# Scores and weighting of an attention mixer two to three pieces later, pooled products in four banks

## The chip, the cores and the metric

One core of a Trainium2 chip runs the whole kernel. The core has five engines, each with its own queue of instructions: TensorE (PE, matrix products; its loads of weights are shown as PEld), VectorE (DVE), ScalarE (ACT), GpSimd (POOL) and SyncE (SP), which here only starts DMAs. DMAs are also started from GpSimd's queue. The metric is the time of the program on the device in microseconds (us), the median of several runs.

## The reference

An encoder of two layers over 256 tokens of 1024 channels, in float32. Each layer has a token mixer and a gated MLP:

```python
def _token_mixer(xn, w_in, w_pool, pool_scale, w_a, w_b, w_o, rel_bias):
    u, q, k, v, g_pool, g_attn = jnp.split(xn @ w_in, SPLITS, axis=-1)
    ug = u.reshape(B, S, POOL_GROUPS, POOL_GROUP_DIM)
    pooled = jnp.stack([_centred_mean(ug[:, :, gi], w) for gi, w in enumerate(POOL_WINDOWS)], axis=2) - ug
    pool_out = jnp.einsum('bsgc,gcd->bsgd', pooled, w_pool).reshape(B, S, POOL_WIDTH) * pool_scale
    ...
    # three groups of four heads with keys at steps of 1, 4 and 16 tokens; per group: logits, lse, p, o
    wts = jax.nn.softmax(jnp.stack(lses, axis=0), axis=0)
    attn = jnp.einsum('gbsh,gbshd->bshd', wts, jnp.stack(outs, axis=0).astype(jnp.float32))
    merged = jax.nn.sigmoid(g_pool) * (pool_out @ w_a) + jax.nn.sigmoid(g_attn) * (attn_out @ w_b)
    return merged @ w_o

for layer in range(DEPTH):
    h = h + _token_mixer(_rmsnorm(h, norm1[layer]), ...)
    h = h + _conv_ffn(_rmsnorm(h, norm2[layer]), ...)
return _rmsnorm(h, norm_f)
```

The softmax over each group followed by the weighting of groups by their denominators is one softmax over the keys of all three groups, and the kernel computes it so.

## The kernel before

**Split operands.** TensorE multiplies operands of a shorter format (fp32r). To keep float32's precision, an operand is split into a high part (a cast on ScalarE) and the rest (a subtraction on VectorE), and a product is three: high by high, high by rest, rest by high. Names ending in `h` and `l`, or `th` and `tl`, are such pairs.

**Weights in pieces.** The class `Weights` (object `W`) brings all weights in one fixed order. A load from memory (`raw`, three buffers, started by SyncE) holds two pieces; a piece is split into `wh` (L208, ScalarE) and `wl` (L210, VectorE), five buffers each, and then multiplied. `W.get()` hands out the next piece, and has the splits made up to `W.look` pieces ahead (3, and 4 in the mixer's attention). `queue_behind(insts, n)` makes the next `n` splits stand behind the given instructions in the queues of ScalarE and VectorE; the last four such requests are kept. A piece in the projections by tokens (`by_tokens`, tile `t_ps`) is twelve products of 512 columns.

**The mixer's order.** After the values `v` and the pooling of `u`, the mixer runs these projections one behind the other: six blocks for queries and keys (four pieces each, `t_ps`), two halves of the pooled branch by `w_a` (`po2`, four pieces each), two halves of the first gate (four pieces each), and then twice a half of the second gate (four pieces, called the third and fourth gate here) with a half of the attention's output by `w_b` (two pieces, operand `at2`).

A block of queries or keys comes out by tokens and is needed by channels, with the tokens regrouped by their steps. `cross` does this over memory: VectorE transposes (L737, tile `qk_rows`, later `turning` for probabilities), SyncE starts a store, and GpSimd starts four loads (L744, tiles `k`, `qk_rows`, `turned_p`). The first two blocks hold queries and keys of the group with step 1; the third to sixth hold those of the two groups with steps 4 and 16, for heads 0 and 1 (third and fourth) and for heads 2 and 3 (fifth and sixth).

**Attention between the pieces.** For each of four heads `hh` (three groups at once), `scores` makes the logits on TensorE (`s_ps`, two tiles) and the softmax on VectorE and ScalarE; `start_turn` sends the probabilities over memory (`cross`); `turn` splits what came back into `pth` (ScalarE, L1098) and `ptl` (VectorE, L1099); `weigh` multiplies them by the values (`o_ps`) and splits the result into `at2` (L1117, L1118). `parts` and `bring` unpack queries and keys. A table written by hand says behind which piece each step stands; place 0 is the first piece of the first block, places 24 to 31 are the pooled branch, 32 to 39 the first gate, and 40 to 43 the third gate:

```python
            21: ((scores, 0), (start_turn, 0)),
            24: ((scores, 1), (start_turn, 1)),
            28: ((turn, 0),),
            29: ((weigh, 0), (scores, 2), (start_turn, 2)),
            30: ((turn, 1),),
            31: ((weigh, 1), (scores, 3), (start_turn, 3)),
            38: ((turn, 3),),
            39: ((weigh, 3), (W.load_one, first_up[l][1])),
```

In this stretch (`manual_schedule`) TensorE, ScalarE and VectorE work in the order of the source; elsewhere a scheduler sets the order. SyncE and GpSimd have an order of their own that the scheduler sets throughout.

**Banks.** Two pools of four PSUM banks: `mmp` (tag `mm`: projections `t_ps`, and the products of the pooled groups `pool_ps`, in the second block) and `acc` (tag `acc`: scores, weighted values, values, residual sums). A block's `t_ps` takes two banks.

**The pooled branch's result** `pa` is copied out of its banks by ScalarE at the end of each half (L1197); its two halves take the places of the rests of queries and keys (`lows`) of heads 0 and 1, and of heads 2 and 3.

**The norm.** The output projection's sum goes into `h` (L468), is squared (L470), scaled (L495, `xn`), turned by TensorE (`xt_ps`) and split into `x` (L507, L508), half of the channels at a time, for tokens `t` = 0 and then `t` = 1.

Of the kernel before, what the change touches and what calls it, by code (L numbers as in the profile page):

```python
# [10 lines left out]
F32 = mybir.dt.float32  # L11
# [6 lines left out]
P = 128  # L18
D = 1024
S = 256  # L20
# [228 lines left out]
def encoder(ctx, tc, x, w_in, w_pool, pool_scale, w_a, w_b, w_o, norm1, norm2, w_up, conv_w,  # L249
            conv_b, w_down, rel_bias, norm_f, onehot, edges, out):  # L250
    nc = tc.nc
    const = ctx.enter_context(tc.tile_pool(name="const", bufs=1))
    wpool = ctx.enter_context(tc.tile_pool(name="weights", bufs=1))
    big = ctx.enter_context(tc.tile_pool(name="big", bufs=1))
# [39 lines left out]
    first_up = []  # L294
# [191 lines left out]
    def to_channels(x2, psum, g):  # L486

        tag = "acc" if psum is acc else "mm"  # L490

        def fin(t, r, xn):
            for n in range(4):
                cc = slice(n * 256, (n + 1) * 256)
                nc.vector.scalar_tensor_tensor(  # L495
                    out=xn[:, cc], in0=h[:, t, cc], scalar=r[:, 0:1], in1=g[:, cc],
                    op0=ALU.mult, op1=ALU.mult,
                )
            for n in range(2):
                pt = psum.tile([P, 4, P], F32, tag=tag, name="xt_ps")  # L500
                ks = slice(4 * n, 4 * n + 4)
                for k in range(4):
                    c0 = (4 * n + k) * P
                    nc.tensor.transpose(pt[:, k, :], xn[:, c0 : c0 + P], ident)
                oh, ol = (x2[:, ks, part, t, :] for part in (0, 1))
                last = [
                    nc.scalar.copy(out=oh, in_=pt),  # L507
                    nc.vector.tensor_sub(out=ol, in0=pt, in1=oh.bitcast(F32)),  # L508
                ]
                if n == 0:  # L510
                    yield
            if t == 1:
                W.queue_behind(last, 6)

        return fin
# [411 lines left out]
    for l in range(DEPTH):  # L927
# [89 lines left out]
        def pool_out(po2):  # L1017
            for j in range(2):
                i, (wh, wl) = W.get()
                for gg in range(2):  # L1020
                    for oc in range(2):
                        ps = mmp.tile([P, 2, S], F32, tag="mm", name="pool_ps")
                        cc = slice(oc * P, (oc + 1) * P)
                        two_sums(
                            pooled[2 * j + gg], 2,
                            (ps, lambda k: wh[:, 2 * gg + k, cc], lambda k: wl[:, 2 * gg + k, cc]),
                        )
                        c = 4 * j + 2 * gg + oc
                        sc = hps[:, l, c : c + 1]
                        po = sm.tile([P, 2, P], F32, tag="u", name="po")  # L1030
                        nc.scalar.mul(out=po, in_=halves(ps[:, 1]), mul=sc)
                        nc.vector.scalar_tensor_tensor(  # L1032
                            out=po, in0=halves(ps[:, 0]), scalar=sc, in1=po, op0=ALU.mult, op1=ALU.add
                        )
# [97 lines left out]
        def bring(half):  # L1132

            a = tmp[:, 0].rearrange("p (a c j) -> p c a j", a=8, c=4)
            nc.scalar.copy(out=q[:, half].rearrange("p c t (a j) -> p c (t a) j", j=32), in_=a)


        steps = {
            9: ((parts, 0),),
            13: ((parts, 1),),  # L1140
            17: ((bring, 0),),
            21: ((scores, 0), (start_turn, 0)),
            24: ((scores, 1), (start_turn, 1)),
            25: ((bring, 1),),
            28: ((turn, 0),),
            29: ((weigh, 0), (scores, 2), (start_turn, 2)),
            30: ((turn, 1),),
            31: ((weigh, 1), (scores, 3), (start_turn, 3)),
            36: ((turn, 2),),
            37: ((weigh, 2),),  # L1150
            38: ((turn, 3),),

            39: ((weigh, 3), (W.load_one, first_up[l][1])),
        }
        places = iter(range(40))

        def step():
            for f, hh in steps.pop(next(places), ()):
# [30 lines left out]
        at2 = big.tile([P, HPG, 2, 2, P], F32R, tag="at2", name="at2")  # L1189


        pa = []
        for n in range(2):
            ps = by_tokens(po2, 4, then=step)
            pa.append(big.tile([P, 2, 512], F32, tag=("q0", "k0")[n], name="pa"))
            for t in range(2):
                nc.scalar.copy(out=pa[n][:, t], in_=ps[t])  # L1197

        def gate(tag):
            ps = by_tokens(x2, 4, then=step if steps else None)  # L1200
# [5 lines left out]
        for n in range(2):  # L1206
            th = gate("q1")
            for t in range(2):
# [1 line left out]
                    out=pa[n][:, t], in0=th[:, t], scalar=1.0, in1=pa[n][:, t],  # L1210
                    op0=ALU.add, op1=ALU.mult,
                )
        assert not steps
        W.look = W.LOOK
        in_order_of_source.close()
        g2 = gain(norm2[l])
        m2 = big.tile([P, 2, KD, 2, P], F32R, tag="m2", name="m2")
        mh, ml = m2[:, 0], m2[:, 1]
        piece, load = first_up[l]
# [1 line left out]
        turned_rows = big.tile([P, 2, 2, 4, 4, 32], F32, tag="xn", name="turned")  # L1221
        for n, cc in enumerate(HALVES):
            th = gate("gates")
            ps = by_tokens(at2, 2, 2)
            ks = slice(4 * n, 4 * n + 4)
            y = turned_rows[:, n]
            z = big.tile([P, 2, 4, 4, 32], F32, tag=("q1", "v0")[n], name="merged")
            for t in range(2):

                with tc.issue_after((turning if t else made[1]).ins) if n + t else ExitStack():  # L1230
                    nc.vector.scalar_tensor_tensor(
                        out=th[:, t], in0=th[:, t], scalar=1.0, in1=ps[t], op0=ALU.add, op1=ALU.mult
                    )
                    nc.vector.tensor_add(out=th[:, t], in0=th[:, t], in1=pa[n][:, t])
                turning, there, made = to_chunks(
                    th[:, t], y[:, t], z[:, t], (mh[:, ks, t], ml[:, ks, t])
                )
# [182 lines left out]
```

## Time and profile before

| | |
|---|---|
| median of 3 runs | 868.67 us (869.62, 864.01, 868.67) |
| the profiled execution | 873.82 us, its span 872.0 us, TensorE's granted clock 0.997 |
| busy | TensorE 855.1 us (98%), weight loads 720.9 (83%), VectorE 664.8 (76%), ScalarE 489.8 (56%), GpSimd 105.9 (12%) |
| memory | 228 GB/s over the span |
| groups with the most time | split rests on VectorE (L210) 331.1 us, casts on ScalarE (L208) 285.4, products `t_ps` of `x` 301.6 and 187.0 |

Line numbers with L are those of the kernel before. "Busy" for TensorE counts overlapping matmuls once. A row of the timeline has the start, the time, engine, line, operation, tile and count, and in brackets the idle time before it and what ended it. A row of waits has the total, the number and the longest.

### The profile page before, as it was taken

The numbers are of one execution on the slowest core, as the hardware profiler recorded it, in microseconds if no ns is written. First come the engines' busy times: TensorE is split into PE (matmuls) and PEld (weight loads), VectorE is DVE, ScalarE is ACT, GpSimd is POOL, SyncE is SP. The second block draws the span as 40 slices with busy tenths as digits, with TensorE's granted clock in tenths as the row PEclk, the third lists the DMA queues.
The fourth block names the chain that finished last, engine by engine and source line by source line (L and its number), as shares of the span: only waits on it lengthen the run. The fifth ranks groups of instructions, "written<-read, shape, count | busy, mean of one in ns | idle before, by whom it ended". The sixth has DMA issues, their size and how long they took to land.

```text
span 872.0 us, 11540 instructions
## 1 busy us (share of the span) xinstructions
PE 855.1 (98%) x4151; PEld 720.9 (83%) x4151; DVE 664.8 (76%) x1018; ACT 489.8 (56%) x759; POOL 105.9 (12%) x226
## 2 busy tenths in 40 slices
PE   9999998999999999999999999998999999999997
PEld 8888787888888888888888878887888888888886
DVE  6998766777756988888855977587666777987884
ACT  6655543455444766666645555454544555765662
POOL 1801122210011211010000012131100122010100
PEclk9999999999999999999999999999999999999999
DMA  9686897895667978665735578988757398776641
GB/s 320 205 256 207 259 295 240 244 319 172 221 210 247 286 226 240 223 226 189 248 113 193 174 259 276 279 262 260 252 199 267 112 315 274 224 229 214 218 145 50
DMA packets 124418, 199.39 MB, mean 229 GB/s; under 512 B 6904, under 2 KB 69056, under 8 KB 124360
## 3 DMA queue, kind: packets, MB, share of 16 engines
q1 hardware_dynamic: 118056, 181.59, 63.3%
q0 software_dynamic: 6144, 16.79, 7.3%
q8 instruction: 33, 0.54, 0.3%
q10 hardware_dynamic: 160, 0.27, 0.1%
q14 instruction: 25, 0.20, 0.1%
HBM read 178.68 MB, written 19.94 MB: 228 GB/s over the span
## 4 chain that ended last, share of the span: by engine, by line
PE 80%; DMA 8%; DVE 6%; issue 2%; ACT 2%; POOL 1%; POOLq 0%; ACTq 0%; DVEq 0%
PE t_ps L690 31%; PE proj_ps L566 18%; PE v_ps L690 6%; PE res_ps L610 6%; PE res_ps L609 6%; PE res_ps L608 6%; DMA k<-crossing 4%; DMA crossing<-qk_rows 4%; PE v_ps L919 3%; DVE wl L210 2%; PE v_ps L826 1%; POOL k L744 1%; PE o_ps L1112 1%; ACT wh L208 1%; DVE qk_rows L737 1%
## 5 line engine op out<-in xcount | busy, mean ns | idle before, releaser
L210 DVE TENSOR_TENSOR wl<-raw,wh 128x1024 fp32r<-128x1024 f32 x274 | 331.1, 1220 | 110.6 <-ACT wh L208 94.5
L208 ACT CAST wh<-raw 128x1024 fp32r<-128x1024 f32 x274 | 285.4, 1051 | 153.5 <-PE t_ps L690 102.1
L690 PE MATMUL t_ps<-wh,x 128*128 128x512 f32 x960 | 301.6, 391 | 0.0
L690 PEld LDWEIGHTS t_ps<-wh,x 128*128 128x128 f32 x960 | 180.7, 188 | 37.6
L690 PE MATMUL t_ps<-wl,x 128*128 128x512 f32 x480 | 187.0, 390 | 0.0
L566 PE MATMUL proj_ps<-x,wh 128*128 128x512 f32 x448 | 106.5, 390 | 0.0
L690 PEld LDWEIGHTS t_ps<-wl,x 128*128 128x128 f32 x480 | 90.4, 188 | 18.6
L566 PEld LDWEIGHTS proj_ps<-x,wh 128*128 128x128 f32 x448 | 83.1, 188 | 16.6
L608 PE MATMUL res_ps<-wh,actq 128*128 128x512 f32 (+1 forms) x184 | 70.1, 381 | 0.0
L609 PE MATMUL res_ps<-wl,actq 128*128 128x512 f32 (+1 forms) x184 | 70.0, 380 | 0.0
L610 PE MATMUL res_ps<-wh,actk 128*128 128x512 f32 (+1 forms) x184 | 69.9, 380 | 0.0
L566 PEld LDWEIGHTS proj_ps<-x,wl 128*128 128x128 f32 x448 | 56.8, 191 | 2.2 <-DVE a L603 0.5
L566 PE MATMUL proj_ps<-x,wl 128*128 128x256 f32 x448 | 57.7, 283 | 0.0
L690 PE MATMUL t_ps<-wh,po 128*128 128x512 f32 x128 | 40.8, 392 | 0.0
L744 POOL DMA_DIRECT2D k<-crossing x32 | 18.8, 594 | 175.1 <-DVE po L1032 70.9
L610 PEld LDWEIGHTS res_ps<-wh,actk 128*128 128x128 f32 x184 | 34.6, 188 | 6.6
L608 PEld LDWEIGHTS res_ps<-wh,actq 128*128 128x128 f32 x184 | 34.6, 188 | 6.4
L609 PEld LDWEIGHTS res_ps<-wl,actq 128*128 128x128 f32 x184 | 34.6, 188 | 6.3
L744 POOL DMA_DIRECT2D zg<-crossing x32 | 18.5, 585 | 170.2 <-DVE y L1323 49.1
L1075 ACT ACTIVATE p<-s,nm 128x512 f32<-128x512 f32 x16 | 11.6, 725 | 34.7 <-DVE nm L1072 32.7
L477 POOL TENSOR_SCALAR ss<-ss 128x1 f32<-128x1 f32 x8 | 1.8, 223 | 229.6 <-ACT junk L470 229.6
L1319 ACT ACTIVATE y<-a,prm 128x256 f32<-128x256 f32 x44 | 25.3, 597 | 6.7 <-DVE a L603 5.2
(204 smaller groups left out, 1214.0 us busy)
## 6 DMA issues: line engine op xcount, KB each, us to landing
raw<-in_w_up_dram SPq DMA_DIRECT2D x44, 1024.0 KB, 6.2
raw<-in_w_in_dram SPq DMA_DIRECT2D x34, 1024.0 KB, 6.1
raw<-in_w_in_dram SPq DMA_DIRECT2D x50, 512.0 KB, 5.2
raw<-in_w_down_dram SPq DMA_DIRECT2D x22, 1024.0 KB, 5.0
raw<-in_w_a_dram SPq DMA_DIRECT2D x8, 1024.0 KB, 10.1
raw<-in_w_o_dram SPq DMA_DIRECT2D x8, 1024.0 KB, 5.5
crossing<-qk_rows SPq DMA_DIRECT2D x12, 512.0 KB, 4.5
crossing<-crossing SPq DMA_DIRECT2D x12, 512.0 KB, 7.7
```

Of the source, the lines that this page charges most:

```text
L208: inst = nc.scalar.copy(out=h, in_=src)
L210: inst = nc.vector.tensor_sub(out=l, in0=src, in1=h.bitcast(F32))
L566: nc.tensor.matmul(out, w(k), x, start=(steps is first and k == 0), stop=(steps is last and k == nk - 1), skip_group_check=turns["rest"],)
L608: nc.tensor.matmul(ps, ah, wh, start=first, stop=False, skip_group_check=on)
L609: nc.tensor.matmul(ps, ah, wl, start=False, stop=False, skip_group_check=on)
L610: nc.tensor.matmul(ps, al, wh, start=False, stop=last, skip_group_check=on)
L690: nc.tensor.matmul(ps, x2[:, 2 * n + j, part, t, :], w[:, j, :], start=(n + m == 0), stop=(n == last and m == 5),)
L737: nc.vector.transpose(out=y[:, t].rearrange("p q c j -> p c q j"), in_=rows[t])
L744: nc.gpsimd.dma_start(out=z[32 * q : 32 * q + 32].rearrange("p a c j -> p a (c j)"), in_=d[:, q].rearrange("(a i) x -> i a x", i=32),)
L919: nc.tensor.matmul(ps[t], a[:, k, t, :], w[:, j, :], start=(k + m == 0), stop=(k == KD - 1 and m == 2),)
L1075: nc.scalar.activation(p, s, AF.Exp, bias=nm[:, 0:1], accum_out=z)
L1319: nc.scalar.activation(y, a, AF.Identity, bias=b, scale=w1)
```

## The change

The table moves each step two or three places (two to three pieces) later, up to place 42, the third of the four pieces of the third gate. In it, `turn` of a head stands ahead of another head's `scores` where they share a place, and the sending of heads 2 and 3 (`start_turn`) stands a place behind their scores. The stretch in the order of the source ends behind the third gate. The copy of the second half of `pa` stands behind head 3's scores. The products of the pooled groups take banks of the pool `acc`. In the norm, one split of weights is queued behind the first half of `t` = 0.

```diff
                 if n == 0:
+                    if t == 0:
+                        W.queue_behind(last, 1)
                     yield
...
-                        ps = mmp.tile([P, 2, S], F32, tag="mm", name="pool_ps")
+                        ps = acc.tile([P, 2, S], F32, tag="acc", name="pool_ps")
...
+        def keep_pa(n):
+            pa.append(big.tile([P, 2, 512], F32, tag=("q0", "k0")[n], name="pa"))
+            for t in range(2):
+                nc.scalar.copy(out=pa[n][:, t], in_=pa_ps[n][t])
...
-            21: ((scores, 0), (start_turn, 0)),
-            24: ((scores, 1), (start_turn, 1)),
-            25: ((bring, 1),),
...
-            31: ((weigh, 1), (scores, 3), (start_turn, 3)),
...
-            39: ((weigh, 3), (W.load_one, first_up[l][1])),
+            24: ((scores, 0), (start_turn, 0)),
+            26: ((scores, 1), (start_turn, 1)),
+            28: ((bring, 1),),
+            31: ((turn, 0), (scores, 2)),
+            32: ((weigh, 0), (start_turn, 2)),
+            33: ((turn, 1), (scores, 3), (keep_pa, 1)),
+            34: ((weigh, 1), (start_turn, 3)),
+            39: ((turn, 2),),
+            40: ((weigh, 2),),
+            41: ((turn, 3),),
+            42: ((weigh, 3), (W.load_one, first_up[l][1])),
```

Where instructions stand now, in three places of layer 0. Numbers in names tell buffers and pieces apart; line numbers of the changed kernel are two higher from L509 on and up to nine higher further down.

The first is TensorE at head 0's scores (`s_ps`). Before, they stand behind piece 43, the second piece of the sixth block:

```order
L690 MATMUL t_ps_1304<-wh43_1244,x2_277 128x512
L1053 MATMUL s_ps_1339<-highs_1052 128x256
L1053 MATMUL s_ps_1339<-lows_1053,highs_1052 128x256
L1053 MATMUL s_ps_1339<-highs_1052,lows_1053 128x256
L1059 MATMUL s_ps_1339<-k_792,q_791 128x128 x2
```

Now they stand behind piece 46, the first piece of the pooled branch:

```order
L692 MATMUL t_ps_1383<-wh46_1305,po2_880 128x512
L1055 MATMUL s_ps_1402<-highs_1052 128x256
L1055 MATMUL s_ps_1402<-lows_1053,highs_1052 128x256
L1055 MATMUL s_ps_1402<-highs_1052,lows_1053 128x256
L1061 MATMUL s_ps_1402<-k_792,q_791 128x128 x2
```

The same products moved past three pieces, 44 to 46.

The second is VectorE at the split of head 1's probabilities (`ptl`). Before, it stands behind the softmax of head 2 (`s_1603` to `p_1615`) and the transposes that send it (`turning`):

```order
L1072 TENSOR_REDUCE nm_1605<-s_1603 128x1
L1066 SCALAR_TENSOR_TENSOR s_1610<-s_ps_1597,bt_82 128x512
L1072 TENSOR_REDUCE nm_1612<-s_1610 128x1
L1079 RECIPROCAL rz_1617<-z_1607 128x1
L1080 TENSOR_SCALAR p_1608<-p_1608,rz_1617 128x512
L1079 RECIPROCAL rz_1620<-z_1614 128x1
L1080 TENSOR_SCALAR p_1615<-p_1615,rz_1620 128x512
L737 STREAM_TRANSPOSE turning_1623<-p_1608 128x4x4x32
L737 STREAM_TRANSPOSE turning_1623<-p_1615 128x4x4x32
L210 TENSOR_TENSOR wl56_1633<-raw28_1505,wh56_1632 128x1024
L1099 TENSOR_TENSOR ptl_1651<-turned_p_1055,pth_1650 128x8x2x32
L210 TENSOR_TENSOR wl57_1655<-raw28_1505,wh57_1654 128x1024
```

Now the split of head 1 (`ptl_1703`) stands ahead of head 3's softmax (`s_1718`), and head 2's transposes stand behind the result of head 0 (`at2`):

```order
L1082 TENSOR_SCALAR p_1636<-p_1636,rz_1641 128x512
L210 TENSOR_TENSOR wl58_1647<-raw29_1543,wh58_1646 128x1024
L1120 TENSOR_TENSOR at2_1381<-o_ps_1664,at2_1381 128x256
L739 STREAM_TRANSPOSE turning_1677<-p_1629 128x4x4x32
L739 STREAM_TRANSPOSE turning_1677<-p_1636 128x4x4x32
L210 TENSOR_TENSOR wl59_1687<-raw29_1543,wh59_1686 128x1024
L1101 TENSOR_TENSOR ptl_1703<-turned_p_1055,pth_1702 128x8x2x32
L1068 SCALAR_TENSOR_TENSOR s_1718<-s_ps_1706,bt_82 128x512
```

The weighing of head 1 on TensorE is a piece behind the scores of head 3 now, where before it stood ahead of them.

The third is VectorE at the norm behind the output projection, for `t` = 0. Before, a split of weights (`wl85`) stands ahead of the first `x`:

```order
L495 SCALAR_TENSOR_TENSOR xn_2179<-h_75,rstd_2301,gain_1914 128x256 x2
L468 TENSOR_TENSOR h_75<-res_ps_2184,h_75 128x512
L495 SCALAR_TENSOR_TENSOR xn_2179<-h_75,rstd_2301,gain_1914 128x256 x2
L468 TENSOR_TENSOR h_75<-res_ps_2185,h_75 128x256
L654 TENSOR_TENSOR h_75<-res_ps_2185,h_75 128x256
L210 TENSOR_TENSOR wl85_2375<-raw42_2238,wh85_2374 128x1024
L508 TENSOR_TENSOR x2_2178<-xt_ps_2335,x2_2178 128x4x128
```

Now it stands behind it, and a row of `h` stands between the first two rows of `xn`:

```order
L495 SCALAR_TENSOR_TENSOR xn_2179<-h_75,rstd_2301,gain_1989 128x256
L468 TENSOR_TENSOR h_75<-res_ps_2184,h_75 128x512
L495 SCALAR_TENSOR_TENSOR xn_2179<-h_75,rstd_2301,gain_1989 128x256 x3
L468 TENSOR_TENSOR h_75<-res_ps_2185,h_75 128x256
L656 TENSOR_TENSOR h_75<-res_ps_2185,h_75 128x256
L508 TENSOR_TENSOR x2_2178<-xt_ps_2335,x2_2178 128x4x128
L468 TENSOR_TENSOR h_75<-res2_ps_2347,h_75 128x256
L210 TENSOR_TENSOR wl85_2375<-raw42_2238,wh85_2374 128x1024
```

The first `x` moved ahead of one split, and the second `xn` behind one row of `h`.

More of the change, by code (lines that the diff above doesn't have):

```diff
@@ L1135, in bring @@
             nc.scalar.copy(out=q[:, half].rearrange("p c t (a j) -> p c (t a) j", j=32), in_=a)
-        steps = {
-            9: ((parts, 0),),
-            13: ((parts, 1),),
-            17: ((bring, 0),),
-            21: ((scores, 0), (start_turn, 0)),
-            24: ((scores, 1), (start_turn, 1)),
-            25: ((bring, 1),),
-            28: ((turn, 0),),
-            29: ((weigh, 0), (scores, 2), (start_turn, 2)),
-            30: ((turn, 1),),
-            31: ((weigh, 1), (scores, 3), (start_turn, 3)),
-            36: ((turn, 2),),
-            37: ((weigh, 2),),
-            38: ((turn, 3),),
-            39: ((weigh, 3), (W.load_one, first_up[l][1])),
+        pa, pa_ps = [], []
+        def keep_pa(n):
+            pa.append(big.tile([P, 2, 512], F32, tag=("q0", "k0")[n], name="pa"))
+            for t in range(2):
+                nc.scalar.copy(out=pa[n][:, t], in_=pa_ps[n][t])
+        steps = {
+            11: ((parts, 0),),
+            15: ((parts, 1),),
+            19: ((bring, 0),),
+            24: ((scores, 0), (start_turn, 0)),
[9 more added lines that the diff above has]
+            42: ((weigh, 3), (W.load_one, first_up[l][1])),
         }
-        places = iter(range(40))
+        places = iter(range(44))
         def step():
@@ L1189, in encoder @@
         at2 = big.tile([P, HPG, 2, 2, P], F32R, tag="at2", name="at2")
-        pa = []
         for n in range(2):
[L1194 to L1197, printed above, removed]
+            pa_ps.append(by_tokens(po2, 4, then=step))
+            if n == 0:
+                keep_pa(n)
         def gate(tag):
@@ L1212, in encoder @@
                 )
[L1213 to L1216, printed above, removed]
         m2 = big.tile([P, 2, KD, 2, P], F32R, tag="m2", name="m2")
@@ L1223, in encoder @@
             th = gate("gates")
+            if n == 0:
+                assert not steps
+                W.look = W.LOOK
+                in_order_of_source.close()
+                g2 = gain(norm2[l])
             ps = by_tokens(at2, 2, 2)
```

## The prediction

> **What bounds the kernel now.** I read the page first, for who is busy, then the waits of TensorE, then TensorE's timeline at each wait, then whatever ended it.
>
> ```profile
> span 872.0 us, 11540 instructions
> PE 855.1 (98%) x4151; PEld 720.9 (83%) x4151; DVE 664.8 (76%) x1018; ACT 489.8 (56%) x759; POOL 105.9 (12%) x226
> ```
> ```profile
> L690 PE MATMUL t_ps<-wh,x 128*128 128x512 f32 x960 | 301.6, 391 | 0.0
> ```
> ```profile
> 200.03 32.69 PE t_ps L690 x144
> ```
>
> TensorE (PE) is the bound: no other engine passes 76%. The chain's row gives its pace: 144 matmuls in 32.69 us are 0.227 us each, or 2.72 us for a piece of twelve. The group's row says that one lasts 0.39 us, so matmuls overlap, and a wait costs the idle time that the profile shows plus the overlap that was lost, 0.39 - 0.23 = 0.16 us. The change moves matmuls and removes none, so all it can win is what TensorE waits:
>
> ```profile
> PE s_ps L1059 <- DMA k<-crossing: 6.2, 3, 3.8
> PE o_ps L1108 <- DVE ptl L1099: 1.8, 2, 0.9
> PE pool_ps L566 <- DVE po L1032: 1.2, 4, 0.4
> PE v_ps L690 <- DVE x L508: 0.8, 2, 0.4
> ```
>
> These are total, times and longest. With 0.16 us for each time, the keys cost 6.2 + 0.5 = 6.7 us, the probabilities 1.8 + 0.3 = 2.1, the pooled products 1.2 + 0.6 = 1.8, and the normalised rows 0.8 + 0.3 = 1.1: 11.7 us in both layers.
>
> **Scores later: the keys.** The largest of the three waits is in layer 0; the last row is head 2's in layer 1, and the 0.7 us that is left of 6.2 is head 0's there.
>
> ```profile
> 131.32 0.28 PE L1053 MATMUL s_ps<-highs,lows 128*128 128x256 f32 x1
> 135.39 0.91 PE L1059 MATMUL s_ps<-k,q 128*128 128x128 f32 x4 [3.79 <-DMA k<-crossing]
> ...
> 137.45 0.77 PE L690 MATMUL t_ps<-wh,x 128*128 128x512 f32 x1
> ...
> 139.22 0.39 PE L690 MATMUL t_ps<-wl,x 128*128 128x512 f32 x1
> ...
> 591.20 0.68 PE L1059 MATMUL s_ps<-k,q 128*128 128x128 f32 x4 [1.66 <-DMA k<-crossing]
> ```
> ```profile
> 131.00:142.00 11.00, 7.21 (x33) 6.17 (x32) 5.31 (x11) 3.26 (x6) 2.31 (x4) 0.84 0.67 232
> ```
> ```profile
> 116.10 8.31 DMA crossing<-qk_rows
> 124.99 1.73 POOL k L744 x3
> 126.71 8.54 DMA k<-crossing
> ```
>
> The granted clock is 0.84 in that window, and from 137.45 to 139.22 four matmuls started in 1.77 us where the pace gives 0.91: another 0.9 us lost behind the wait. No such stretch follows the wait of 1.66 us, so I charge a wait its own length, and 0.9 more only when it is as long as this one. The Trainium skill, "TensorE: Matmul & The Clock Gate", HAM oscillation — how this bites in real kernels, says that an idle gap over about 3.4 us puts TensorE back to half clock. The trace agrees (3.79 us did, 1.66 us did not); by the page's half clock over one such window my estimate would be 1.7 us instead of 0.9.
>
> The keys left SyncE's queue at 116.10 and were in place at 135.25, 19.2 us later. In the changed kernel they leave where they did (the block of projections that makes them has not moved, and comes 0.9 us earlier with the pooled waits gone), while head 0's scores stand three pieces later: 3 x 2.72 = 8.2 us against a wait of 3.79. That leaves 4.4 us of slack in layer 0 and 7.5 in layer 1. Head 2's wait (1.66 us) gets two pieces, 5.4 us, and its keys also leave earlier: their transposes no longer stand behind head 0's softmax on VectorE. I take all of it: **-6.7 and -0.9**.
>
> **Splits ahead of other scores: the probabilities.**
>
> ```profile
> 169.78 1.19 DVE L210 TENSOR_TENSOR wl<-raw,wh 128x1024 fp32r<-128x1024 f32 x1
> 170.88 0.68 DVE L1099 TENSOR_TENSOR ptl<-turned_p,pth 128x512 fp32r<-128x512 f32 x1
> ```
>
> Head 1's split on VectorE (`ptl`) stood behind head 2's whole softmax and started at 170.88; TensorE wanted it at 170.6. Now the split stands ahead of head 3's scores, and the weighing a piece plus a set of scores behind it (2.72 + 1.6 us), so the wait goes: **-2.1**. What pays is the next transposes of probabilities: heads 2 and 3 now turn behind the previous head's `at2` split. The price by VectorE's groups:
>
> ```profile
> L1066 DVE SCALAR_TENSOR_TENSOR s<-s_ps,bt 128x512 f32<-128x512 f32 x16 | 11.0, 686 | 10.4 <-PE s_ps L1059 10.3
> L1072 DVE TENSOR_REDUCE nm<-s 128x1 f32<-128x512 f32 x16 | 11.0, 686 | 0.6
> L1080 DVE TENSOR_SCALAR p<-p,rz 128x512 f32<-128x512 f32 x16 | 7.9, 497 | 0.6
> L737 DVE STREAM_TRANSPOSE turning<-p 128x512 f32<-128x512 f32 x16 | 10.4, 688 | 0.0
> L210 DVE TENSOR_TENSOR wl<-raw,wh 128x1024 fp32r<-128x1024 f32 x274 | 331.1, 1220 | 110.6 <-ACT wh L208 94.5
> ```
>
> A head's softmax is 2 x (0.69 + 0.69 + 0.50) = 3.8 us and its two transposes 1.4; a piece's split is 1.22 of each 2.72 us. Two heads of layer 0 are tight, the first (split at 159.21, weighing at 161.75) and the last:
>
> ```profile
> 173.13 0.36 PE L1053 MATMUL s_ps<-highs 128*128 128x256 f32 x1
> ```
> ```profile
> 159.21 0.69 DVE L1099 TENSOR_TENSOR ptl<-turned_p,pth 128x512 fp32r<-128x512 f32 x1
> ...
> 178.49 1.30 DVE L737 STREAM_TRANSPOSE turning<-p 128x512 f32<-128x512 f32 x2
> ...
> 196.41 0.69 DVE L1099 TENSOR_TENSOR ptl<-turned_p,pth 128x512 fp32r<-128x512 f32 x1 [0.86 <-ACT pth L1098]
> ```
> ```profile
> 195.76 0.62 ACT L1098 CAST pth<-turned_p 128x512 fp32r<-128x512 f32 x1 [1.46 <-DMA turned_p<-turning]
> ```
> ```profile
> 161.75 0.28 PE L1108 MATMUL o_ps<-pth,vh 128*128 128x256 f32 x1
> ...
> 198.26 0.28 PE L1108 MATMUL o_ps<-pth,vh 128*128 128x256 f32 x1
> ```
>
> From head 3's scores (173.13) to weighing (198.26) were 25.1 us, and the split ended at 197.10, 1.2 us ahead. Now nine pieces, one set of scores and two weighings lie between: 9 x 2.72 + 3 x 1.6 = 29.3 us, 4.2 more. The transposes ended 6.7 us after the scores began; now they wait for the weighing of head 1, a piece after the scores: 1.6 + 2.7 + 1.6 to its end, about 0.8 for ScalarE's copy, a `wl` split and the `at2` split (1.6), then 1.4: 9.7 us, 3.0 more. Slack 1.2 + 4.2 - 3.0 = 2.4 us. Head 0's split ended at 159.90, 1.9 us ahead, and goes from eight pieces and two sets of scores to eight and three, 1.6 us more. Its four loads on GpSimd's queue stand behind those of the keys of heads 2 and 3 now, whose four issues take 2.3 us (0.58 each, by 1.73 for three), so it may give up 0.7: 1.2 to 3.5 us of slack. Heads 1 and 2 get a piece more and stand looser. I cost all this at nothing; what hides it is TensorE's projections, and if the cover is too short, TensorE waits the difference, head by head.
>
> VectorE's backlog: two heads' softmax and transposes (10.4 us) two pieces apart leave splits late, but a split is made four pieces (10.9 us) before its use and itself takes 1.0 on ScalarE and 1.2 on VectorE, so it can be about 8 us late. Two pieces and two sets of scores hold 8.6 us, of which 2.4 are splits: the backlog is about 4 us. Nothing.
>
> **Pooled products in four banks.**
>
> ```profile
> 88.15 0.72 PE L566 MATMUL pool_ps<-pl,wh 128*128 128x512 f32 x2 [0.23 <-DVE po L1032]
> ...
> 89.48 0.50 PE L566 MATMUL pool_ps<-pl,wl 128*128 128x256 f32 x2 [0.38 <-DVE po L1032]
> ```
>
> Products waited for VectorE to empty the two banks that the projections left them. Four give a whole further piece (2.72 us) against 0.4: **-1.8**. The second half's `pa` copies move behind head 3's scores; the banks they hold are wanted again only two pieces later, 5.4 us, against an exponential and two copies of some 3.
>
> **The rows queued behind the first half.** The new queueing puts one split of weights behind the norm's first copies:
>
> ```profile
> 251.75 0.88 DVE L495 SCALAR_TENSOR_TENSOR xn<-h,rstd,gain 128x256 f32<-128x256 f32 x2 [0.74 <-POOL rstd L482]
> 252.55 0.68 DVE L468 TENSOR_TENSOR h<-res_ps,h 128x512 f32<-128x512 f32 x1
> ...
> 254.60 1.22 DVE L210 TENSOR_TENSOR wl<-raw,wh 128x1024 fp32r<-128x1024 f32 x1
> 255.74 0.69 DVE L508 TENSOR_TENSOR x<-xt_ps,x 128x512 fp32r<-128x512 f32 x1
> ```
> ```profile
> 253.15 0.60 PE L504 MATMUL xt_ps<-ident,xn 128*128 128x128 f32 x4
> ...
> 256.48 1.19 PE L690 MATMUL v_ps<-v,x 128*128 128x512 f32 x4 [0.40 <-DVE x L508]
> ```
>
> Without the 1.22 us in front, `x` is there by 255.4 and the wait of 1.1 us in two layers goes. But the `h` row now stands between the first two `xn` rows, so the second ends at about 253.2 where TensorE takes it at 253.15: between 0.1 and 0.3 us lost in each layer, since the row in between is 0.68 long and 0.5 of it was spare. I take 0.2: **-1.1 + 0.4 = -0.7**.
>
> **The sum.** -6.7 - 0.9 - 2.1 - 1.8 - 0.7 = -12.2. The profiled execution took 873.82 us (span 872.0 and 1.8 around it), so the changed one's would take 861.6. The runs shown have median 868.67, 5.2 below the profiled one. If that gap is a cost that any profiled execution has, the changed median is 868.67 - 12.2 = 856.5. If it is DMA waits that were longer in that one execution, the change removes them in any case, and it is 861.6. The fastest run bounds this: at 864.01 it is only 2.4 above 861.6, but must hold the waits that no DMA ends, 2.1 + 1.8 + 0.7 = 4.6, so at least 2.2 of the gap belong to the profiled execution: 856.5 to 859.4. I take 859, near the upper end, as the runs differ by 5.6 us, the size of the keys' wait, and the two slower ones must hold most of it.
>
> **Rivals.**
>
> A, new small waits. Heads 0 and 3 have the slack worked out above, 1.2 to 3.5 us, with a DMA chain that took 17.3 us in this trace from the transposes to the cast (178.49 to 195.76), and 19.2 for the keys. Chains 3 to 5 us longer cost 1 to 3 us in each layer, and sometimes the clock's 0.9: 861 to 867. For it: head 3 waited for its DMA already. Against: every chain got more time than it lost, but for head 0's 0.7. Chance 0.22.
>
> B, slower than before. ScalarE is a queue: head 0's cast `pth` now stands ahead of head 2's exponentials. If its probabilities come late, ScalarE stops, and with it the softmax behind it, the weight splits and, when their 8 us are used up, TensorE's projections. To end above the median from 859 it must cost 9.7 us, 4.85 in each layer, of which 0.9 is the clock after a long wait: TensorE waits 4 us. With some 2 us of slack on a chain of 17.3 us, that begins at a chain of 23.3 us. At 27 us TensorE waits 7.7, and 859 + 2 x (7.7 + 0.9) = 876. For it: the keys' chain in layer 0 shows that DMA can stretch. Against: to 19.2 us, the longest in the trace, in its busiest stretch. Chance 0.06.
>
> C, the change doesn't reach the wait: the keys' chain moves along with its readers. It speaks for it that this is what a busy DMA did in layer 0 (19.2 us); against it, that the sender's place is fixed and 8.2 us exceed 3.79 twice over. Only the other terms remain, 868.67 - 4.6 = 864. Chance 0.07.
>
> **How the numbers follow.** The forecast (856 to 861.5) has 0.65. One part in a hundred of 868.67 is 8.7 us, about what a measurement of this kernel can tell from no change; that bound is at 860.0 and lies inside the forecast. Some 0.48 of its 0.65 are under it and nothing of A or C above it but 0.02: faster 0.5. Slower by over 1% (877.4) takes a chain a little over 27 us, the upper part of B: 0.05. The same: 0.45. The range runs from 855.5, a microsecond below the constant gap's 856.5 (the 0.4 taken for the norm may be nothing, and the overlaps are rounded), to 867, the end of A.
>
> **What would show it.** Each wait has its row. TensorE's list of waits should lose the keys, `ptl` and `po`, and `x`; its busy share should pass 99%; the granted clock should be 1.00 in the window that now has 0.84. On the norm's term: a wait of `xt_ps` for `xn` of 0.1 to 0.3 us. If `o_ps` waits for `pth` or `turned_p`, A or B is at work, and how much of ScalarE's idle time is ended by that DMA says which. I am wrong if waits are gone and the time is not: then TensorE's pace itself, 0.227 us, has changed.

## The result, and the profile after

| kernel | runs | median, us | lowest to highest |
|---|---|---|---|
| before | 4 | 868.26 | 864.01 to 869.62 |
| changed | 4 | 858.18 | 857.66 to 859.23 |

The ratio is 0.9894, with a 95% interval of 0.9858 to 0.9930. The profiled execution of the changed kernel took 859.23 us. Here are its first lines:

```profile
span 857.4 us, 11532 instructions
PE 849.2 (99%) x4151; PEld 718.2 (84%) x4151; DVE 663.8 (77%) x1018; ACT 487.7 (57%) x759; POOL 107.1 (12%) x226
```

VectorE and ScalarE do what they did; TensorE is busy for 6 us less with the same matmuls, as fewer of them run slowly or without overlap behind a wait. TensorE's waits (engine, line, what was waited for: total, times, longest) are down to two, and none of the four groups of before is among them (`gain_ps`, at the very start, is in the list of before too, with the same 0.8):

```profile
PE proj_ps L568 <- DVE a L605: 1.1, 1, 1.1
PE gain_ps L395 <- PEq L1411: 0.8, 1, 0.8
```

The same window that had a granted clock of 0.84 (the first of the last three columns), and TensorE's timeline where head 0's scores now stand:

```profile
131.00:142.00 11.00, 11.00 (x57) 9.37 (x56) 7.92 (x13) 4.84 (x8) 2.31 (x4) 1.00 0.90 275
```
```profile
136.09 0.39 PE L692 MATMUL t_ps<-wh,po 128*128 128x512 f32 x1
136.32 0.28 PE L1055 MATMUL s_ps<-highs 128*128 128x256 f32 x1
136.43 0.28 PE L1055 MATMUL s_ps<-lows,highs 128*128 128x256 f32 x1
136.55 0.28 PE L1055 MATMUL s_ps<-highs,lows 128*128 128x256 f32 x1
136.67 0.61 PE L1061 MATMUL s_ps<-k,q 128*128 128x128 f32 x4
```

The products of `k` and `q` follow within 0.12 us, with no idle time in brackets. To put numbers on all waits alike I added up, over the whole trace, by how much each matmul started later than the pace of its kind (those above 0.12 us): 14.6 us before, 1.6 us after, so 13.0 of the 14.6 us between the two spans lie in places with a name. The terms of the prediction are 12.7 of them. The rest is 1.6 us that went in the first microseconds, which the change doesn't touch, less the new 1.2 us of `proj_ps` (below).

### The profile page after: what moved, and what is told of

The parts are those of the page before. It is cut to its first block, busy times and chain, and to the rows that moved or that the text cites. A ratio compares the mean times of both kernels' runs of the same rounds, so it can differ in the third digit from the quotient of the medians.

```text
span 857.4 us, 11532 instructions
## 1 busy us (share of the span) xinstructions
PE 849.2 (99%) x4151; PEld 718.2 (84%) x4151; DVE 663.8 (77%) x1018; ACT 487.7 (57%) x759; POOL 107.1 (12%) x226
## 4 chain that ended last, share of the span: by engine, by line
PE 96%; DMA 2%; DVE 1%; ACT 0%; POOL 0%; issue 0%; POOLq 0%; DVEq 0%; ACTq 0%
PE t_ps L692 44%; PE proj_ps L568 18%; PE v_ps L692 6%; PE res_ps L611 6%; PE res_ps L612 6%; PE res_ps L610 6%; PE v_ps L921 3%; PE v_ps L828 1%; PE pool_ps L568 1%; DMA zg<-crossing 1%; PE o_ps L1114 1%; PE s_ps L1061 1%; DMA raw<-in_w_up_dram 1%; PE s_ps L1055 1%; PE o_ps L1110 1%; PE xt_ps L504 1%
## 5 line engine op out<-in xcount | busy, mean ns | idle before, releaser
L1362 ACT CAST actq<-g 128x256 fp32r<-128x256 f32 x44 | 17.5, 402 | 23.2 <-DVE g L1351 22.5
```

Of the source, the lines that this page charges most:

```text
L1362: nc.scalar.copy(out=ah, in_=g)
```

## The experiments

All were timed beside runs of the kernel before, whose median on the three chips was 869.98, 869.72 and 869.37 us. The ratio is to those runs. "Late starts" is the sum just described, from the one profile of each.

| kernel | median | lowest to highest | ratio (95%) | late starts, us |
|---|---|---|---|---|
| before, again | 868.83 | 865.35 to 872.60 | 0.9977 (0.9951 to 1.0003) | 9.9 |
| banks alone | 871.61 | 867.56 to 875.39 | 1.0015 (0.9989 to 1.0041) | 13.7 |
| request alone | 868.78 | 866.88 to 871.54 | 0.9986 (0.9962 to 1.0009) | 13.6 |
| table alone | 860.99 | 860.16 to 864.14 | 0.9894 (0.9860 to 0.9928) | 2.2 |
| changed, again | 857.74 | 857.43 to 858.12 | 0.9862 (0.9837 to 0.9887) | 0.3 |
| table and banks | 859.80 | 858.18 to 862.24 | 0.9887 (0.9861 to 0.9913) | 4.4 |
| table and banks, again | 858.38 | 857.83 to 860.63 | 0.9879 (0.9857 to 0.9902) | 0.9 |
| head 0's scores at 21 | 867.00 | 865.09 to 870.71 | 0.9968 (0.9949 to 0.9987) | 8.5 |
| head 0's scores at 22 | 858.88 | 857.54 to 862.16 | 0.9892 (0.9864 to 0.9919) | 0.7 |
| splits behind scores | 864.77 | 864.17 to 866.85 | 0.9950 (0.9932 to 0.9969) | 6.7 |
| keys alone | 867.38 | 865.04 to 873.19 | 0.9974 (0.9951 to 0.9997) | 8.1 |
| weighing early | 866.19 | 863.27 to 869.68 | 0.9962 (0.9941 to 0.9982) | 7.3 |

For all of them the span less the late starts is 855 to 858 us. What makes these kernels differ by more than that is TensorE's waiting and the slow clock behind it. The sum leaves out what comes less than 0.12 us late, so it holds little of a slow clock over short products; that matters for the keys alone (below).

**The kernel before, a second time** (no edit).

> The kernel of before once more, for a second profiled execution. Theory 1: the waits that a DMA ends differ from one execution to the next, the others do not. The idle time shown for `ptl`, `po` and `x` comes again within 0.1 us of 1.8, 1.2 and 0.8; that for the keys is another than 6.2 (between 2 and 6); the four slow microseconds at the start, which cost 1.6 us in the first profile (5 to 9 us), may be missing; and the profiled time then lies 1 to 4 us above the median, not 5.5. Rival: a profiled execution costs 5.5 us more than a timed one, whatever it waits for. Then the profiled time is 873 to 874 again, with the keys' wait near 6.2. Time against before: 1.00.

It was profiled at 868.28 us, below the median of its own runs. TensorE's waits and timeline:

```profile
PE s_ps L1059 <- DMA k<-crossing: 3.1, 3, 1.5
PE o_ps L1108 <- DVE ptl L1099: 1.8, 2, 0.9
PE pool_ps L566 <- DVE po L1032: 1.2, 4, 0.4
PE v_ps L690 <- DVE x L508: 0.8, 2, 0.4
```
```profile
130.92 0.68 PE L1059 MATMUL s_ps<-k,q 128*128 128x128 f32 x4 [0.66 <-DMA k<-crossing]
...
557.88 0.35 PE L1059 MATMUL s_ps<-k,q 128*128 128x128 f32 x1 [1.53 <-DMA k<-crossing]
...
585.67 0.57 PE L1059 MATMUL s_ps<-k,q 128*128 128x128 f32 x3 [0.90 <-DMA k<-crossing]
```

Three of the four groups are as before to the tenth; only the keys' has halved, and layer 0's part of it went from 3.79 to 0.66. So in these two executions the waits that engines end are the same, that for a DMA is not, and the 5.2 us of the first are no constant price of a profiled execution.

**The banks alone** (before, with one line of the change).

```diff
-                        ps = mmp.tile([P, 2, S], F32, tag="mm", name="pool_ps")
+                        ps = acc.tile([P, 2, S], F32, tag="acc", name="pool_ps")
```

> Before, with the pooled products in the four banks of `acc` and nothing else. Theory 1: the four waits of `pool_ps` for `po` go (1.8 us by start-to-start times: 0.39 + 0.53 in layer 0, 0.39 + 0.51 in layer 1), and all that follows, the keys' departure too, comes 0.9 us earlier in each layer, so the keys' wait stays as long as it was. Time 866.5, ratio 0.998. Rival: the gain is given back at the keys, whose wait grows by up to 0.9 us a layer, since their transfer hangs on DMA and not on TensorE. Then the time stays at 868.

The four waits for `po` went, and the kernel was not faster: the interval runs from 1.0 us faster to 3.6 slower, and 1.8 faster lies outside it. The profile has two waits for keys, of 5.9 us together, with a granted clock of 0.62 (131 to 140 us) and 0.76 (560 to 567 us) over the windows behind them, where the first profile of before has a slow window behind one wait only. The time fits the rival, but as this wait differs by 3 us between two profiles of one kernel, a single trace can't show where the 1.8 us went.

**The request alone** (before, with `W.queue_behind(last, 1)` in the norm), and **the table alone** (the changed kernel without the banks and the request).

> Before, with the one new request to queue a split behind the norm's first half and nothing else. Theory 1 (the prediction's): the wait of `v_ps` for `x` goes (0.57 us a layer start to start), and `xt_ps` waits 0.1 to 0.3 us for the second `xn`: between -0.4 and -1.0 us, 867.6 median. Rival (from the profile after, which shows no wait of `xt_ps`): the row of `h` between the two `xn` costs nothing: -1.1 us, 867.1. A second rival: the split that was put back is late for the projections, and a wait for `wl` of up to 0.5 us appears.

> Before, with the new table (steps two to three places later, splits ahead of other scores, the order of the source to the end of the third gate, the second `pa` behind head 3's scores), and with the pooled products and the norm as before. Theory 1: the keys' and the `ptl` waits go, the `po` and `x` waits stay with 1.2 and 0.8 us of idle time: of 10.1 us won by the whole change 1.8 + 1.1 = 2.9 are missing, the time is 861.1 (ratio 0.992). Rival: the parts need each other (the 0.9 us from the pooled banks let the keys leave earlier): part of the keys' wait stays and the time is 862 to 864.

VectorE's timeline at the norm of layer 0, with the request alone:

```profile
249.75 0.88 DVE L495 SCALAR_TENSOR_TENSOR xn<-h,rstd,gain 128x256 f32<-128x256 f32 x2 [0.73 <-POOL rstd L482]
250.54 0.69 DVE L468 TENSOR_TENSOR h<-res_ps,h 128x512 f32<-128x512 f32 x1
251.14 0.88 DVE L495 SCALAR_TENSOR_TENSOR xn<-h,rstd,gain 128x256 f32<-128x256 f32 x2
...
252.60 0.68 DVE L508 TENSOR_TENSOR x<-xt_ps,x 128x512 fp32r<-128x512 f32 x1
...
253.93 1.23 DVE L210 TENSOR_TENSOR wl<-raw,wh 128x1024 fp32r<-128x1024 f32 x1 [0.29 <-ACT wh L208]
```

and with the table alone:

```profile
243.14 0.48 DVE L495 SCALAR_TENSOR_TENSOR xn<-h,rstd,gain 128x256 f32<-128x256 f32 x1 [0.73 <-POOL rstd L482]
243.54 0.68 DVE L468 TENSOR_TENSOR h<-res_ps,h 128x512 f32<-128x512 f32 x1
...
245.99 0.68 DVE L508 TENSOR_TENSOR x<-xt_ps,x 128x512 fp32r<-128x512 f32 x1
246.58 1.22 DVE L210 TENSOR_TENSOR wl<-raw,wh 128x1024 fp32r<-128x1024 f32 x1
```

With the request alone the two `xn` run together, as before, and the first `x` stands ahead of the split. With the table alone the row of `h` stands between the two `xn`, and the first `x` stands ahead of the split without being asked to. So the row of `h`, which I had put down to the request, comes with the table, and the earlier `x` comes with either (presumably the scheduler chooses anew behind the longer stretch in the order of the source; that is only argued). Either edit by itself removes the wait for `x`; neither profile has it. The request alone can't be told from no change in time.

The table alone has only the `po` waits left of the four groups:

```profile
PE pool_ps L566 <- DVE po L1032: 1.2, 4, 0.4
PE gain_ps L395 <- PEq L1409: 0.8, 1, 0.8
```

It is 9.0 us below before and brings most of the gain.

**The changed kernel again, and without the request** (table and banks, twice).

> The changed kernel once more, beside the next three on one chip. Theory: what scatters the runs of before (865.65 to 875.35 in 29 runs) is the wait for the keys, which a DMA ends; the changed kernel has none left, so its runs lie within 3 us of each other, around 858 to 860, and the profile has the idle times of before's four groups at zero. Rival: the scatter belongs to the chip and the runs; then these scatter by 8 to 10 us as well.

> The changed kernel without the request to queue a split behind the norm's first half. Theory 1 (from the profile of the table alone, which has no wait for `x` though it lacks the request): the table already moves the first `x` ahead of the split, the request adds nothing, and the time is that of the changed kernel within 0.3 us. Rival (the prediction's): the request is what removes the wait of 0.57 us a layer; the time is 1.1 us longer.

> Once more the changed kernel without the request to queue a split in the norm. It stood at 858.2 to 858.7 in three runs and at 860.9 to 862.2 in three others, where nine runs of the changed kernel have one above 859. Theory 1: the request does nothing for the time, and the upper three are runs in which the weights of the up projection came late (the profile among them shows 1.56 and 1.42 us behind them); then most of the runs lie at 858.0 to 859.0 now. Rival: without the request half of the runs wait for those weights again, and the median is 859 to 861.

The five runs of the changed kernel lie within 0.7 us of each other, where before scattered by 8. On this chip it is 12.0 us faster than before, 1.38%. Against the table alone, the banks bring 1.2 to 2.6 us now by the medians (860.99 to 859.80 and 858.38, on three chips), and 0.6 to 1.3 by the ratios to the runs of before beside each, whose intervals overlap; what is shown is that the `po` waits are gone from the profiles. Of the twelve runs without the request, four are above 860, of nine with it none. The profile of one of the four (861.49) shows what came late. TensorE's waits, and ScalarE's timeline at the first of those two of `proj_ps`:

```profile
PE proj_ps L566 <- DVE a L603: 2.6, 2, 1.4
```
```profile
302.56 1.05 ACT L208 CAST wh<-raw 128x1024 fp32r<-128x1024 f32 x1 [2.11 <-DMA raw<-in_w_up_dram]
303.51 0.66 ACT L602 COPY a<-proj_ps 128x256 f32<-128x256 f32 x2
```

`proj_ps` waits for VectorE's `a`, that for ScalarE's copy of it, and the copy stands in ScalarE's queue behind a cast that stood 2.11 us for its weights. (TensorE's list has one more wait that the first profile of the changed kernel hasn't, 1.0 us of `v_ps` in the first microseconds.) The wait of `proj_ps` is also in three profiles of kernels that have the request: the first of the changed kernel (1.1 us), the request alone (1.2, with the old table) and head 0's scores at 21 (0.5). So the request doesn't exclude it, and the new table isn't needed for it. Whether it makes it rarer stays open: four of twelve against none of nine can be chance, and the other eight runs lie within 1.0 us of 857.74.

**Head 0's scores three and two pieces earlier** (the changed kernel with one line split; 22 instead of 21 in the second).

```diff
-            24: ((scores, 0), (start_turn, 0)),
+            21: ((scores, 0),),
+            24: ((start_turn, 0),),
```

> The changed kernel with head 0's scores three pieces earlier, at the place that they had before (the sending of its probabilities stays). Theory 1: the keys' wait comes back, though shorter than before, as the keys now leave 2 us earlier: the products of `k` and `q` would start 8.2 us earlier, at 128.5 in layer 0 and 550.3 in layer 1, and by the changed kernel's profile the last load lands at 129 to 131 and at 553: idle 0.5 to 2.4 and about 2.9 us, with up to 1 us of slower clock behind each, so 3.5 to 7 us more than the changed kernel, and runs that scatter by more than 3 us. Rival: the keys come earlier when they are read earlier (the transfer only fills the time it has); then nothing changes, within 0.5 us.

> The changed kernel with head 0's scores two pieces earlier instead of three. The run with three pieces showed the keys in place at 131.2 in layer 0 and 553.4 in layer 1; the products of `k` and `q` would start at 131.2 and 553.0. Theory 1 (the keys' arrival is set by their sender and by DMA, and the place of the scores only says how much of it shows): a wait of 0 to 1 us is left in most runs, the median is 858.5 to 860.5, 6 to 8 us under that with three pieces, and the runs scatter by 2 to 4 us. Rival (the arrival moves with its readers): as with three pieces, 865 to 867.

Three pieces earlier, 9.3 of the 12.0 us are gone again, more than the 3.5 to 7 that I had expected. TensorE's waits and timeline, and its windows behind the two waits:

```profile
PE s_ps L1061 <- DMA k<-crossing: 4.5, 2, 2.5
```
```profile
131.19 0.68 PE L1061 MATMUL s_ps<-k,q 128*128 128x128 f32 x4 [2.54 <-DMA k<-crossing]
...
557.28 0.68 PE L1061 MATMUL s_ps<-k,q 128*128 128x128 f32 x4 [1.92 <-DMA k<-crossing]
```
```profile
130.00:137.00 7.00, 5.81 (x24) 5.07 (x25) 4.40 (x9) 2.58 (x5) 2.30 (x4) 0.76 0.73 253
556.00:563.00 7.00, 5.72 (x24) 4.85 (x25) 4.31 (x9) 2.57 (x5) 2.31 (x4) 0.76 0.85 279
```

Two pieces earlier there is no wait for keys in the profile, and the median is 1.1 us above the changed kernel's on another chip (the ratios are 0.9892 and 0.9862), with runs up to 862. So the first piece pays most; the other two presumably take late arrivals, which this one profile doesn't show. Had the arrival moved with its readers (rival C), the second kernel would have waited like the first.

**The splits behind the other scores again** (the changed kernel with two places turned round).

```diff
-            31: ((turn, 0), (scores, 2)),
+            31: ((scores, 2), (turn, 0)),
-            33: ((turn, 1), (scores, 3), (keep_pa, 1)),
+            33: ((scores, 3), (turn, 1), (keep_pa, 1)),
```

> The changed kernel with the splits of the probabilities of heads 0 and 1 behind the scores of heads 2 and 3 again, at the same places. Theory 1: VectorE gets to `ptl` only behind a softmax, which ends at 164.0 and 173.0 in layer 0 of the changed kernel, so `ptl` ends about 0.7 us later, at 164.9 and 173.7, where the weighing starts at 163.0 and 171.8: four waits of some 2 us, 8 us in all, and up to 13 with the slower clock behind each. Rival: the weighing stands late enough in any case, and the order of split and scores is worth nothing: within 0.5 us of the changed kernel.

It is 7.0 us above the changed kernel. TensorE's waits and timeline:

```profile
PE o_ps L1110 <- ACT pth L1100: 2.7, 4, 0.7
PE o_ps L1110 <- DVE ptl L1101: 1.7, 4, 0.4
```
```profile
163.98 0.38 PE L1110 MATMUL o_ps<-pth,vh 128*128 128x256 f32 x1 [0.68 <-ACT pth L1100]
164.79 0.39 PE L1110 MATMUL o_ps<-ptl,vh 128*128 128x256 f32 x1 [0.43 <-DVE ptl L1101]
```

Four times 0.84 + 0.70 us, start to start, are 6.2. The cast `pth` is late too, as it stands behind the other head's exponentials on ScalarE; I had counted VectorE alone. The two halves of each wait are short, and no slow clock follows (1.00 over 163 to 170 us).

**The keys alone** (before, with head 0's scores and the sending of its probabilities two pieces later, and nothing else).

```diff
-            21: ((scores, 0), (start_turn, 0)),
+            23: ((scores, 0), (start_turn, 0)),
```

> Before, with nothing but head 0's scores (and the sending of its probabilities) two pieces later, at 23 instead of 21. Theory 1: the keys' wait of head 0 goes in both layers, since two pieces (5.4 us) are more than any wait seen there (3.95); head 0's probabilities lose what the wait gave them, some 6 us in layer 0 against a slack of about 5, so `o_ps` waits up to 1 us for them there. Ratio to before 0.990 to 0.994 (864 to 861 us), that is most of what the whole change brings, with the waits for `ptl`, `po`, `x` and head 2's keys as they were. Rival: the later scores only move the wait to the probabilities, in full: then `o_ps` waits 3 us or more for `pth` and the time is 867 or above.

The keys' wait of head 0 went, and only 2.0 us with it. TensorE's waits, ScalarE's timeline in layer 0, and TensorE's timeline and window there:

```profile
PE o_ps L1108 <- ACT pth L1098: 1.6, 1, 1.6
PE pool_ps L566 <- DVE po L1032: 1.2, 4, 0.4
PE o_ps L1108 <- DVE ptl L1099: 1.0, 2, 0.6
```
```profile
164.93 0.62 ACT L1098 CAST pth<-turned_p 128x512 fp32r<-128x512 f32 x1 [2.60 <-DMA turned_p<-turning]
```
```profile
165.60 0.38 PE L1108 MATMUL o_ps<-pth,vh 128*128 128x256 f32 x1 [1.57 <-ACT pth L1098]
166.33 0.39 PE L1108 MATMUL o_ps<-ptl,vh 128*128 128x256 f32 x1 [0.34 <-DVE ptl L1099]
```
```profile
164.00:171.00 7.00, 5.09 (x29) 4.86 (x29) 3.27 (x5) 1.94 (x3) 2.30 (x4) 0.76 0.64 219
```

The late one is head 1, not head 0: its scores now stand a piece behind head 0's, its probabilities come over the same queues, and its weighing, which the keys' wait had held back, comes too early. The rival was right in the time and in the mechanism: taking the first wait away uncovers the second, and ScalarE itself stands still for 2.6 us. In layer 0 TensorE's part is 1.57 + 0.34 us and not the rival's 3, but the granted clock behind it is 0.76, and head 1's last eight products take 1.91 us where head 0's took 1.05. The table alone, which weighs later too, has no wait of `o_ps` in its profile.

**The weighing early** (the changed kernel, heads 0, 2 and 3 split and weighed two pieces earlier).

```diff
+            29: ((turn, 0),),
+            30: ((weigh, 0),),
...
+            37: ((turn, 2),),
+            38: ((weigh, 2),),
+            39: ((turn, 3),),
...
+            40: ((weigh, 3),),
```

> The changed kernel with the splits and the weighing of heads 0, 2 and 3 two pieces earlier (scores stay): it measures the slack of rival A. Two pieces are 5.4 us. By the prediction's slack (head 0: 1.2 to 3.5 us, head 3: 2.4) `o_ps` would wait 2 to 4 us for head 0 and 3 us for head 3 in each layer, with slower clock behind them 10 to 16 us in all: 868 to 874. By the changed kernel's profile (head 0: last load landed at about 155.4, cast at 157.1, split ready at 159.1, weighing at 163.0; head 3: landed at about 190, cast at 192.7, ready at 194.7, weighing at 197.2) the slack is 5.6 and 5 us: waits of 0 to 1 us each, 858 to 861.

TensorE's timeline, and ScalarE's, at head 3 in layer 0:

```profile
193.98 0.38 PE L1110 MATMUL o_ps<-pth,vh 128*128 128x256 f32 x1 [2.15 <-ACT pth L1100]
194.71 0.39 PE L1110 MATMUL o_ps<-ptl,vh 128*128 128x256 f32 x1 [0.34 <-DVE ptl L1101]
```
```profile
193.31 0.62 ACT L1100 CAST pth<-turned_p 128x512 fp32r<-128x512 f32 x1 [5.61 <-DMA turned_p<-turning]
```

Head 3 waits 2.31 + 0.61 = 2.9 us start to start in layer 0 and 3.0 in layer 1, when it comes 5.4 earlier: its slack was 2.5 us, the prediction's 2.4, and not the 5 that I read from the profile of the changed kernel afterwards, where the last landing shows only as a span of durations and no wait marks it. The time, 866.19 us, lies between the two forecasts. Head 0's weighing in layer 0 starts at 155.82 here and at 163.02 in the changed kernel, 7.2 us earlier and not 5.4, as head 2's scores no longer stand ahead of it; it waits 0.31, so its slack was about 6.9, not 1.2 to 3.5.

## Why the prediction was right

- **TensorE's waits decide.** This held in every run. The sum of -12.2 us meets -12.0 on the second chip and -10.1 on the first. That it comes so close is partly luck: 7.6 us of it are the keys of one execution, and with the 3.6 of the second profile of before the sum would be -8.2.
- **The keys, -6.7 - 0.9.** The mechanism is shown by head 0's scores at 21. The size is no constant: 7.6 us in the first profile of before, 3.6 in the second, and 9.3 by the timed runs when three pieces are taken back from head 0 alone. The step that failed is the clock's: I charged 0.9 us only behind a wait as long as 3.79. With head 0's scores at 21, behind waits of 2.54 and 1.92 us, the late starts of `t_ps` come to 1.15 and 1.55, and the clock also fell behind a wait shorter than the 1.66 us that I took as harmless (last section).
- **The probabilities, -2.1.** The two waits went, and nothing took their place. That the order on VectorE and ScalarE carries it is shown by turning it round.
- **The banks, -1.8.** The `po` waits go wherever the banks are changed. In time this shows only where the keys no longer wait, and there weakly (1.2 to 2.6 by the medians, 0.6 to 1.3 by the ratios); by themselves the banks won nothing in the kernel before.
- **The norm, -0.7.** The wait went, -1.1. The predicted wait of `xt_ps` for `xn` is not there, so the 0.4 for the row of `h` was wrong; and the request got a credit that the table earns without it.
- **The covers.** Nothing taken at zero cost turned up as a wait in the two profiles of the changed kernel; their one new wait, of `proj_ps`, is in the up projection, which the prediction didn't look at. Head 3 has the 2.4 us that were worked out. Head 0's bounds were too low, for two reasons. I had taken off up to 2.3 us for its four loads, which stand behind those of the keys on GpSimd's queue; GpSimd's timeline after shows that they waited for their own store there, not for the queue:

```profile
143.16 2.30 POOL L746 DMA_DIRECT2D k<-crossing  x4 [8.16 <-DMA crossing<-qk_rows]
146.29 2.30 POOL L746 DMA_DIRECT2D turned_p<-turning  x4 [0.83 <-DMA turning<-turning]
```

And I had taken the time at which head 0's split ran for the time at which its probabilities were there. Before, ScalarE's cast ahead of that split has no idle time in brackets, so no row shows that it waited for them:

```profile
157.94 0.62 ACT L1098 CAST pth<-turned_p 128x512 fp32r<-128x512 f32 x1
```

Head 3's cast, whose bound held, was marked as waiting for its DMA (1.46 us).

- **From the profile to the median.** Of the two readings of the 5.2 us gap, the constant one fell. The profiled execution of before had long DMA waits and, besides, a slow start, which I had not looked at. TensorE's timeline there, before:

```profile
7.60 1.63 PE L826 MATMUL v_ps<-m,xuh 128*128 128x512 f32 x3
```

and after:

```profile
6.54 0.94 PE L828 MATMUL v_ps<-m,xuh 128*128 128x512 f32 x3
```

In the trace's record of the clock, full clock begins at 9.40 us before and at 4.68 after; the change doesn't touch that. The start alone is 1.6 of the 2.4 us by which the 861.6 for the profiled execution was too high (859.23 measured, and 857.62 in the second). For the median, 859 was taken near the upper end of 856.5 to 859.4; measured were 858.18 and 857.74, nearer the middle.
- **Rivals.** A, B and C did not come. What B and A rest on exists: with the keys alone, ScalarE stood for a DMA and TensorE behind it. There the late head was 1, whose slack I had not worked out, as the full table gives it a piece more.

## What to carry to other kernels

A wait that a DMA ends can differ from one execution to the next (3.79 and 0.66 us here): look at it in two executions before giving it a price, and look for it in the scatter of the times. A wait early in a chain can cover those behind it, so move the readers of the next transfer by as much as the first wait gives back, and work out each one's slack before. If a scheduler sets the order around an edit, show by the rows which edit moved which instruction before crediting it.

## What the runs showed of the hardware that I had not expected

TensorE's clock falls behind shorter waits than I had taken. With the request alone, layer 1's wait of 1.88 us was followed by a granted clock (third column from the end) of 0.72:

```profile
587.77 0.68 PE L1061 MATMUL s_ps<-k,q 128*128 128x128 f32 x4 [1.88 <-DMA k<-crossing]
```
```profile
587.00:593.00 6.00, 5.23 (x22) 4.46 (x23) 4.08 (x9) 2.56 (x6) 0.00 (x0) 0.72 0.79 263
```

Yet 2.15 us did nothing at head 3's weighing in layer 0 of the early one, and 2.19 in layer 1 did:

```profile
193.00:200.00 7.00, 5.68 (x31) 4.81 (x32) 5.60 (x7) 6.04 (x9) 0.00 (x0) 1.00 0.26 100
618.00:626.00 8.00, 6.36 (x27) 5.65 (x28) 5.00 (x7) 5.34 (x8) 0.00 (x0) 0.79 0.22 82
```

Behind the waits for keys of 1.53 and 1.66 us in the two profiles of before it stayed at 1.00; behind head 1's 1.57 us with the keys alone (0.34 more a product later) it was 0.76. So between 1.5 and 2.2 us it fell behind some waits and not behind others, and the length of the wait alone doesn't decide. In the traces' record of the clock each of these falls is a stretch of 3.41 us at half clock; behind the longer wait with the banks alone it is 6.83 us. The Trainium skill, "TensorE: Matmul & The Clock Gate", HAM oscillation — how this bites in real kernels, gives gaps over about 3.4 us as the limit; here waits of 1.57, 1.88 and 1.92 us were enough, and the measurement decides.
